# SSD's output product as pairs of blocks in seven products, with h stored and fetched back

## The chip, the cores and the metric

The kernel runs on one core of one Trainium2 chip. The metric is the device time of one execution in microseconds (us), the median of three runs. The profile is that of one execution, taken by the hardware profiler; its times are measured from the start of that execution's span. PE is the matrix engine and PEld its weight load, DVE, ACT and POOL are the vector, scalar and GpSimd engines, and SP is the engine whose queue issues nearly all DMAs here.

## The reference, cut to what matters

One decoder layer over 1024 tokens of width 1024. Two token mixers work on the same normed and modulated input h: a Mamba-2 SSD branch and a differential attention branch. Sigmoid gates merge them, and a gated convolution FFN follows.

```
h = rms_norm(x, pre_norm1_w) * (1.0 + sc1) + sh1
z, xbc, dt_raw, q, k, v, gates = split(h @ w_in)
y_ssd = ssd_branch(z, xbc, dt_raw, ...)         # ends in y * silu(z), group norm, * ssd_norm_w
y_att = diff_attention_branch(q, k, v, ...)     # 16 q and k heads of 64, 8 v heads of 128
gate_ssd, gate_att = split(sigmoid(gates))
merged = gate_ssd * (y_ssd @ w_ssd_o) + gate_att * (y_att @ w_attn_o)
mix = merged @ w_out
```

The product that the change rewrites is y_ssd @ w_ssd_o, 1024 x 1024 by 1024 x 1024. The first 16 of the 64 dimensions of each q and k head are rotated by rope.

## The kernel before, in words

**Numbers in two parts.** Each float32 operand of a large product is a pair: a high part in float32r and a low part, the rest. A product of two pairs is three matmuls (high by high, high by low, low by high). ACT writes the high part, DVE the low one (`split`, lines 93 to 95).

**h.** `hT[k][half]` holds rows 128k to 128k+127 of h transposed, for one half of the tokens (512), high and low side by side: 16 tiles of 512 KB, which stay in SBUF from the first stage to the end of the attention. All large tiles are taken from 43 slots of 4 KB a partition (`Slots`): `get` takes the slot that has been free longest, and a new tile waits until all that was done with the slot's old tile is done.

**Two forms of product.** `block_half` (lines 120 and 121, through `mm3`, lines 113 to 118) multiplies a 128-column block of a weight by h or y for one half of the tokens in 24 matmuls of 512 columns; a block of both halves is 48. The projection of xBC and some others run in `pairs` instead: two blocks of the weight and the halves of the tokens and of the inner dimension form a 2 x 2 product of blocks, done in seven products (Strassen's scheme in Winograd's form) of 12 matmuls each, 84 for two blocks. It needs sums of the weight's quarters (`x_sum`), their high and low parts (`x_split`, issued ahead by `x_ahead`), and seven right sides `HX[...]` from h: b11, b21 and b22 are pieces of h itself, t1 to t4 are differences. `x_mms` issues one product of 12 matmuls; the results are put together in PSUM banks X, Y, Z, by ACT copies and DVE additions.

**The order.** Within a stage the order on PE, DVE, ACT and SP is the order of the code (`tc.manual_schedule`), so each of these engines' instructions, SP's DMAs among them, waits in line. In the attention stage SP is not in that list, and its DMAs are placed by the planner.

**Stages around the change.** From 250 to 344 us z, then to 515 the SSD scan, chunk by chunk in 16 units (`u`), with V's projection (`v_stream`, from line 940) filling PE in between. V's weight comes in two halves of columns of four pieces each; at the switch to the second half `split_v` gives the pieces' high parts, and the low ones come a step later. `sum_dn` runs four steps per unit of W_down's sums in the background, up to unit 11, except for the first two steps of units 7 and 8. `chunk_state` ends a unit: it adds to `prev`, which the next unit's `chunk_out` reads.

Then come the lines that the change rewrites. `seq` is a list of twelve weight blocks: q and k blocks 0 and 1 (the rotated dimensions), then the eight blocks of w_ssd_o. `fetch_seq` loads one, `split_seq` splits it. For each of the four q and k blocks (numbered 0 to 3 in `seq`) PE runs `block_half` for both halves of the tokens; between them, `turn_y` (lines 1179 to 1188) transposes y, which the scan wrote to DRAM (`yd`), 128 columns by 512 tokens at a time through PSUM banks wa, wb, wa, wc in turn, where ACT writes the high part with ssd_norm_w and DVE the low part. y's first half of tokens sits in four tiles `yr`, and the second half is loaded into the same four once the first is transposed. `rope` takes a finished block of q or k: ACT copies it from PSUM, DVE shuffles and multiplies, POOL multiplies, DVE adds, ACT writes the high and DVE the low part, and `store_qk` writes both to DRAM in 16 DMAs on SP.

Then the eight blocks of w_ssd_o (the loop over j): two `block_half` from `yT`, and DVE multiplies the result by the gate (`gth`, loaded from `gsd`), which is stored (`msd`). At j of 3 and 4 `load_qk` fetches the q and k of the first two heads, each in one DMA of 512 KB for q and four of 256 KB for k's high and low part.

The attention starts behind it: `dense_stream` gives PE 24-matmul halves of the other q, k and gate blocks, a step of three matmuls at a time; 14 steps, then the first heads' `scores`, then a fixed mixture of both.

## Time and profile before

| what | value |
|---|---|
| median of 3 runs (lowest to highest) | 1854.49 us (1852.49 to 1855.08) |
| the profiled execution's own time | 1853.7 us |
| its span | 1851.9 us |
| PE busy in the span | 1824.3 us |
| granted TensorE clock | 0.999 |
| DMA, mean over the span | 174 GB/s |

How to read it: rows of a timeline give start and length in us, engine, line, operation, what is written and read, and in brackets how long the engine stood idle before, and what released it. A row of stages gives busy times between two moments. SPq is SP's queue, which issues DMAs; rows of issues give a DMA's size and the time from issue to landing. Matmuls overlap in part, so their distance from start to start is what they cost.

### The profile page before, as it was taken

What the parts mean: (1) busy time and instruction counts of PE and PEld (TensorE: products, weight loads), DVE (VectorE), ACT (ScalarE), POOL (GpSimd) and SP (SyncE); (2) the same over time, 40 slices, a digit from 0 to 9 for tenths busy, and PEclk for the clock granted to TensorE, in tenths of its full rate; (3) what the DMA queues carried; (4) which work ended last, traced back from release to release, by engine and by line L of the source; (5) the groups of instructions that cost most, each with busy time, mean ns of one, the idle gap of its engine ahead of it and who ended that gap; (6) DMA issues with size and microseconds to landing.
All of it is one profiled execution on the core that took longest, in us unless ns stands there. A gap on an engine that the chain in (4) does not pass through costs nothing.

```text
span 1851.9 us, 24405 instructions
## 1 busy us (share of the span) xinstructions
PE 1824.3 (99%) x8974; PEld 1526.9 (82%) x8974; DVE 1292.3 (70%) x1980; ACT 889.3 (48%) x1720; POOL 143.4 (8%) x128
## 2 busy tenths in 40 slices
PE   6999999999999999999999999999999999999998
PEld 4888899987888888888888888888888888888887
DVE  6777867689654257777667464487898888876555
ACT  6644543455532136565556232565545454454542
POOL 0000000255411000000000100000000000000001
PEclk9999999999999999999999999999999999999999
DMA  8365367687646856566734654122333322378754
GB/s 336 130 216 182 102 209 236 222 305 263 239 130 180 253 140 179 155 172 164 194 114 139 236 197 178 51 98 103 102 120 108 103 97 100 108 231 291 247 171 165
DMA packets 130218, 322.57 MB, mean 174 GB/s; under 512 B 14882, under 2 KB 38834, under 8 KB 130099
## 3 DMA queue, kind: packets, MB, share of 16 engines
q1 hardware_dynamic: 129138, 317.86, 52.7%
q0 software_dynamic: 960, 3.15, 0.5%
q8 instruction: 71, 1.16, 0.3%
q14 instruction: 49, 0.39, 0.1%
HBM read 225.79 MB, written 95.17 MB: 173 GB/s over the span
## 4 chain that ended last, share of the span: by engine, by line
PE 86%; DVE 5%; ACT 3%; DMA 3%; issue 1%; SPq 1%; POOL 0%; DVEq 0%; POOLq 0%; ACTq 0%
PE upx L1742 4%; PE upx L1743 4%; PE upx L1741 4%; PE o L1435 3%; PE upy L1742 2%; PE upy L1741 2%; PE upy L1743 2%; PE z L117 2%; PE z L118 2%; PE z L116 2%; PE dx L2105 2%; PE dy L2106 2%; PE dy L2105 2%; PE dy L2104 2%; PE dx L2106 2%; PE at L1422 2%
## 5 line engine op out<-in xcount | busy, mean ns | idle before, releaser
L1741 PE MATMUL upx<-t,wu_t 128*128 128x512 f32 x264 | 103.1, 391 | 0.5 <-DVE cv L2169 0.4
L1742 PE MATMUL upx<-t,wu_t 128*128 128x512 f32 x264 | 102.9, 390 | 0.2 <-DVE t L1859 0.2
L1743 PE MATMUL upx<-t,wu_t 128*128 128x512 f32 x264 | 102.7, 389 | 0.0
L1715 ACT ACTIVATE wu_t<-sab 128x512 fp32r<-128x512 f32 x57 | 34.1, 627 | 128.0 <-DVE sab L1732 128.0
L1423 ACT COPY aT<-at 128x512 f32<-128x512 f32 (+2 forms) x96 | 46.1, 480 | 96.2 <-PE at L1422 96.2
L1435 PEld LDWEIGHTS o<-vt,aT 128*128 128x128 f32 x576 | 75.3, 191 | 9.2 <-ACT aT L1423 4.6
L95 DVE TENSOR_TENSOR g_lo<-gst,g_hi 128x1024 fp32r<-128x1024 f32 (+1 forms) x42 | 47.5, 1135 | 49.1 <-ACT g_hi L94 45.4
L1435 PE MATMUL o<-vt,aT 128*128 128x128 f32 x576 | 80.9, 276 | 0.4 <-ACT aT L1423 0.2
L94 ACT ACTIVATE g_hi<-gst 128x1024 fp32r<-128x1024 f32 (+1 forms) x42 | 41.4, 989 | 63.5 <-DMA gst<-gld_s 35.8
L1396 DVE TENSOR_REDUCE nmx<-sc 128x1 f32<-128x640 f32 (+3 forms) x64 | 65.6, 1024 | 2.2
L1376 PE MATMUL sc<-kst,qst 128*128 128x512 f32 (+2 forms) x192 | 63.8, 341 | 0.0
L1377 PE MATMUL sc<-klo,qst 128*128 128x512 f32 (+2 forms) x192 | 63.3, 346 | 0.0
L1759 DVE SCALAR_TENSOR_TENSOR ug<-cg,vec,ug 128x1023 f32<-128x1023 f32 (+1 forms) x44 | 56.3, 1280 | 6.1 <-ACT ug L1758 5.3
L1741 PEld LDWEIGHTS upx<-t,wu_t 128*128 128x128 f32 x264 | 49.6, 188 | 11.7 <-DVE cv L2169 1.3
L1742 PEld LDWEIGHTS upx<-t,wu_t 128*128 128x128 f32 x264 | 49.6, 188 | 10.6 <-DVE t L1859 0.5
L1743 PEld LDWEIGHTS upx<-t,wu_t 128*128 128x128 f32 x264 | 49.6, 188 | 10.3
L1719 DVE TENSOR_TENSOR wu_t<-sab,wu_t 128x512 fp32r<-128x512 f32 x57 | 39.3, 690 | 26.6 <-ACT wu_t L1715 26.6
L1759 DVE SCALAR_TENSOR_TENSOR uv<-cv,vec,uv 128x1023 f32<-128x1023 f32 (+1 forms) x44 | 56.2, 1277 | 0.9 <-ACT uv L1758 0.9
L1412 DVE RECIPROCAL rsm<-ssum 128x2 f32<-128x2 f32 x64 | 10.6, 165 | 62.5 <-ACT p L1409 35.2
L1414 DVE SCALAR_TENSOR_TENSOR p<-p,coef,p 128x128 f32<-128x128 f32 (+3 forms) x64 | 52.4, 818 | 2.2
L2225 POOL TENSOR_TENSOR rsf<-rsf,nhalf 128x1 f32<-128x1 f32 x8 | 5.2, 656 | 624.8 <-DVE rsf L2224 624.8
L2104 PE MATMUL dx<-wdt_hi,g_hi 128*128 128x512 f32 x132 | 51.3, 389 | 0.0
(537 smaller groups left out, 5919.7 us busy)
## 6 DMA issues: line engine op xcount, KB each, us to landing
adas<-in_w_ada SPq DMA_DIRECT2D x32, 512.0 KB, 5.2
wdr<-in_w_down SPq DMA_DIRECT2D x22, 512.0 KB, 5.8
wtd<-wds SPq DMA_DIRECT2D x22, 512.0 KB, 3.1
wuf<-in_w_up SPq DMA_DIRECT2D x22, 512.0 KB, 3.5
gld_s<-gsum SPq DMA_DIRECT2D x22, 512.0 KB, 2.8
gst<-gld_s SPq DMA_DIRECT2D x20, 512.0 KB, 5.0
wdt_raw<-wtd SPq DMA_DIRECT2D x20, 512.0 KB, 4.9
wuv<-in_w_up SPq DMA_DIRECT2D x19, 512.0 KB, 3.5
```

The lines of the kernel that those rows point to most:

```text
L1376: T.matmul(sc[:, n0:n1], qs_[s][:, tsl], ks_[s][:, n0:n1], start=True, stop=False)
L1377: T.matmul(sc[:, n0:n1], qs_[s][:, tsl], kl[s][:, n0:n1], start=False, stop=True)
L1396: V.reduce_max(nmx[:, bq, s : s + 1], sc[:, :L], axis=AX.X, negate=True)
L1414: V.scalar_tensor_tensor(pr[0][:, :L], pr[1][:, :L], coef[:, bq : bq + 1], pr[0][:, :L], op0=ALU.mult, op1=ALU.add)
L1435: T.matmul(po_of[j, grp][:, qi, :], at[:, k, :], vt[j % 2][:, kt, :], start=(kt == 0), stop=(kt == i))
L1741: T.matmul(out_, wh, xh_, start=(k == 0 and first), stop=False, skip_group_check=not first)
L1742: T.matmul(out_, wh, xl_, start=False, stop=False, skip_group_check=not first)
L1743: T.matmul(out_, wl, xh_, start=False, stop=(k == end), skip_group_check=not first)
L1759: V.scalar_tensor_tensor(u[:, d:], c_[:, : S - d], fw[:, 2 - d : 3 - d], u[:, d:], op0=ALU.mult, op1=ALU.add)
L2104: T.matmul(o, gh[:, kk, tsl], wh, start=(k == 0 and not more), stop=False, skip_group_check=more)
L2105: T.matmul(o, gh[:, kk, tsl], wl, start=False, stop=False, skip_group_check=more)
L2106: T.matmul(o, gl[:, kk, tsl], wh, start=False, stop=(k == KF - 1), skip_group_check=more)
```

## The change

- In xBC's pairs 4 to 6 the twelve tiles of h that have no copy in DRAM are stored to `hd`, one with every other product; the four others have one already.
- At V's second half the low parts come with the next even step instead of the step after the high part. `sum_dn` does nothing in unit 7, and two more steps in units 0 and 1.
- The q and k blocks run in another order of halves (block 3's first half before block 2's second), y's transposes (0 to 7 for the first half of the tokens, 8 to 15 for the second) stand behind them in the order of `turns`, y's second half is loaded into four tiles of its own, and y's pieces b11, b21 (high and low) and the plain pieces y11, y21, y12, y22 take the place of `yT`. From them come t1 to t4 and b22.
- The eight blocks of w_ssd_o become four pairs appended to `pairs`, in seven products each. The gate's multiplication follows the parts of the result as they are ready (`out_so`); its tiles are loaded two at a time.
- Rope of blocks 2 and 3 is cut into steps between the pairs' products, its stores behind the last step.
- h leaves SBUF after the q and k blocks and is loaded back by `h_back` in the last two pairs: three tiles behind product 3 (counted from 0) of the third pair, two behind its product 5, then 4, 4 and 3 behind products 0, 1 and 2 of the last pair. `fetch(0)` and `fetch(1)`, the dense stream's first weights, move from that stream into the last pair, and `load_qk` for the first two heads goes behind product 3 of the last pair.

```diff
+    h_out = [(k, 0) for k in range(KD)] + [(k, 1) for k in range(KH, KD)]
+    hd = {kh: dp.tile([P, S], F32, tag=f"hd{kh[0]}_{kh[1]}", name=f"hd{kh[0]}_{kh[1]}") for kh in h_out}
+    hd |= {(k, 1): h12d[k] for k in range(KH)}
...
+                if 4 <= m < 7 and p % 2 == 0:
+                    k, half = h_out[4 * (m - 4) + p // 2]
+                    SP.dma_start(hd[k, half], hT[k][half].rearrange("p h t -> p (h t)").bitcast(F32))
...
-                    if (vh == 0 and i == 7 and k > 1) or (vh == 1 and i == 0 and k < 2):
-                        if k % 2 == 0:
+                    if k % 2 == 0 and ((vh == 0 and i == 7 and k > 0) or (vh == 1 and i == 0 and k < 4)):
+                        if v_low:
+                            v_low.pop()()
+                            if k == 4 and vh == 0:
+                                v_raw.append(fetch_v(1, 3))
+                        if v_raw:
                             v_low.append(split_v(1, (k // 2 - 1) % 4, v_raw.pop(0)))
...
-        if u not in (7, 8) or n > 1:
+        if u == 7 or (u == 8 and n < 2):
+            return
+        for _ in range(2 if u < 2 and n == 3 else 1):
...
+        if half == 0:
+            n, src = (("b11", y11), ("b21", y21))[c]
+            A.activation(HX[n][kk][:, 0, :], ps, AF.Copy, scale=nw)
+            A.activation(part(src, kk), ps, AF.Copy, scale=nw)
+            lo_of(n, kk, src)
+        elif c == 0:
+            V.scalar_tensor_tensor(part(y12, kk), ps, nw, part(y11, kk), op0=ALU.mult, op1=ALU.subtract)
+        else:
+            A.activation(part(y22, kk), ps, AF.Copy, scale=nw)
...
+    def rope(n, q_):
+        V.stream_shuffle(sw, q_, perm)
+        yield
+        G.tensor_tensor(q_, q_, ropc, op=ALU.mult)
         V.tensor_tensor(sw, sw, rops, op=ALU.mult)
-        V.tensor_tensor(qf, qf, sw, op=ALU.add)
-        split(hi, lo, qf)
-
-    turns = [((0, 1), (2, 3, 4)), ((5, 6, 7), ()), ((0, 1), (2, 3)), ((4, 5), (6, 7))]
+        yield
+        V.tensor_tensor(q_, q_, sw, op=ALU.add)
+        yield
+        A.activation(hi, q_, AF.Copy)
+        yield
+        V.tensor_tensor(lo, q_, hi.bitcast(F32), op=ALU.subtract)
+        yield
+        store_qk(*seq[n], hi, lo)
...
+    def h_back(n):
+        for _ in range(n):
+            half, k = divmod(n_back[0], KD)
+            n_back[0] += 1
+            hT[k][half] = new_hl(f"hb{k}_{half}")
+            SP.dma_start(hT[k][half].rearrange("p h t -> p (h t)").bitcast(F32), hd[k, half])
...
+    turns = {(0, 0): (0, 4, 1), (0, 1): (5, 2, 6), (1, 0): (3, 7, 8, 12), (1, 1): (9, 13, 10), (2, 0): (14, 11, 15)}
...
+        for n, half in ((0, 0), (0, 1), (1, 0), (1, 1), (2, 0), (3, 0), (2, 1), (3, 1)):
+            if half == 0:
+                if n < 2:
+                    fetch_seq(n + 2)
+                ps_of[n] = ps_mm(f"{seq[n][0]}p{seq[n][1]}")
+            block_half(ps_of[n][:, half, :], seq_w[n], hT, half)
+            if (n, half) in ((0, 0), (1, 0), (2, 0)):
+                split_seq(n + 1)
+            if (n, half) == (1, 0):
+                x_load()
+            if half == 0 and n in (1, 2):
+                rope_in(n - 1, qf)
+                old = rope(n - 1, qf)
+                for _ in range(5):
+                    next(old)
+            for i in turns.get((n, half), ()):
+                if i == 8:
+                    SL.put(*yrs[0])
+                    y12, y22 = [[SL.get(f"ys{n_}_{i_}", F32, (P, 2, HALF)) for i_ in range(2)] for n_ in ("12", "22")]
+                turn_y(i % KD, i // KD)
+            if (n, half) == (0, 1):
+                for q in range(4):
+                    SP.dma_start(yrs[1][q], yd[4 + q])
...
+        for m in range(m0, len(pairs)):
+            for p in range(7):
+                if p == 3:
+                    bank["Y"] = ps_wa(f"sy{m}")
+                x_mms(m, p)
...
+                if m > m0 and (m, p) != (m0 + 1, 0):
+                    if next(ropes, True) and m == m0 + 2 and p == 4:
+                        SL.put(hi, lo)
+                if m == len(pairs) - 2:
+                    if p == 3:
+                        SL.put(ropc, rops, qf, qf2, sw)
+                        gthb = [SL.get(f"gthb{i}") for i in range(2)]
+                        for n in range(2):
+                            SP.dma_start(gthb[n], gsd[j + 2 + n])
+                        h_back(3)
+                    elif p == 5:
+                        h_back(2)
+                if last:
+                    if p == 0:
+                        fetch(0)
+                    elif p == 3:
+                        SL.put(*sab)
+                        fetch(1)
+                    SL.put(*HX[order[p][0]])
+                    if p < 3:
+                        h_back((4, 4, 3)[p])
+                    elif p == 3:
+                        qst, kst, klo = [[[SL.get(f"{n}0_{s}", F32R) for s in range(2)]] for n in ("qst", "kst", "klo")]
+                        for i in range(2):
+                            load_qk(i, qst[0][i], kst[0][i], klo[0][i])
...
-        fetch(0)
-        fetch(1)
```

More of the change, by code (lines that the diff above doesn't have):

```diff
@@ L1086, in load_y @@
             SP.dma_start(yr[q], yd[4 * half + q])
-    seq = [("w_q", 0), ("w_k", 0), ("w_q", 1), ("w_k", 1)] + [("w_ssd_o", j) for j in range(8)]
+    seq = [("w_q", 0), ("w_k", 0), ("w_q", 1), ("w_k", 1)]
     seq_w = {}
@@ L1198, in split_seq, with rope_in @@
             split(*seq_w[n], raw)
[L1201 to L1209 removed]
+    def rope_in(n, dst):
+        A.activation(dst, ps_of[n].rearrange("p h t -> p (h t)"), AF.Copy, scale=qscale[seq[n][0]])
@@ new lines, in rope @@
+    def rope(n, q_):
+        V.stream_shuffle(sw, q_, perm)
+        yield
+        G.tensor_tensor(q_, q_, ropc, op=ALU.mult)
+        V.tensor_tensor(sw, sw, rops, op=ALU.mult)
+        yield
[6 more added lines that the diff above has]
+        store_qk(*seq[n], hi, lo)
+    blocks = [(kind, b) for b in (3, 4, 5) for kind in ("w_q", "w_k")] + [("ga", 0)]
@@ new lines, with fetch @@
+    blocks += [(kind, b) for b in (6, 7) for kind in ("w_q", "w_k")] + [("ga", g) for g in range(1, 8)]
+    raws, splits = {}, {}
+    def fetch(n):
+        if n < len(blocks):
+            kind, j = blocks[n]
+            raws[n] = wp.tile([P, KD, P], F32, tag="wraw", name=f"{kind}{j}_raw", bufs=3)
+            SP.dma_start(raws[n].rearrange("p k c -> p (k c)"), a["w_gate"][8 + j] if kind == "ga" else a[kind][j])
+    def h_back(n):
[4 more added lines that the diff above has]
+            SP.dma_start(hT[k][half].rearrange("p h t -> p (h t)").bitcast(F32), hd[k, half])
@@ L1261 @@
+        out_so(1, first, xbank[m]["X"])
+        SP.dma_start(msd[7], cgv[1])
+    SL.put(*gths, *cgv, *evs_x)
+    singles.close()
+    pairs_of_banks = ExitStack()
+    pmm = pairs_of_banks.enter_context(tc.tile_pool(name="pmm3", bufs=1, space=bass.MemoryType.PSUM))
     vt = [SL.get(f"vt{i}", F32, (P, 8, P)) for i in range(2)]
@@ L1275 @@
     sqt = const("sqt", [P, 4])
-    blocks = [(kind, b) for b in (3, 4, 5) for kind in ("w_q", "w_k")] + [("ga", 0)]
-    blocks += [(kind, b) for b in (6, 7) for kind in ("w_q", "w_k")] + [("ga", g) for g in range(1, 8)]
     emitted = {"scores": 0, "values": 0}
-    raws, splits = {}, {}
     finished.clear()
-    def fetch(n):
-        if n < len(blocks):
-            kind, j = blocks[n]
-            raws[n] = wp.tile([P, KD, P], F32, tag="wraw", name=f"{kind}{j}_raw", bufs=3)
-            SP.dma_start(raws[n].rearrange("p k c -> p (k c)"), a["w_gate"][8 + j] if kind == "ga" else a[kind][j])
     def split_later(n):
```

187 lines of the change are left out of this document (128 added, 59 removed).

## The prediction

> **What bounds the kernel now.** I read the page's totals and its chain first, then a table of stages, then the rows of the product itself.
>
> ```profile
> span 1851.9 us, 24405 instructions
> ...
> PE 1824.3 (99%) x8974; PEld 1526.9 (82%) x8974; DVE 1292.3 (70%) x1980; ACT 889.3 (48%) x1720; POOL 143.4 (8%) x128
> ...
> PE 86%; DVE 5%; ACT 3%; DMA 3%; issue 1%; SPq 1%; POOL 0%; DVEq 0%; POOLq 0%; ACTq 0%
> ```
>
> PE is busy for all but 28 us of the span, and 86% of the chain that ended last is PE's: whatever takes matmuls off PE is worth their issue time, and whatever makes PE wait costs the whole wait.
>
> ```profile
> 193.00:212.00 19.00, 19.00 (x86) 15.73 (x85) 16.11 (x20) 10.14 (x16) 0.00 (x0) 1.00 0.37 112
> ...
> 566.00:653.00 87.00, 86.88 (x383) 71.58 (x383) 25.86 (x32) 12.21 (x15) 3.43 (x1) 1.00 0.75 226
> 653.00:664.00 11.00, 11.00 (x53) 9.16 (x52) 2.74 (x5) 0.60 (x1) 0.00 (x0) 1.00 0.12 48
> ```
>
> The columns are the stretch and its length, the busy time of PE, weight load, DVE, ACT and POOL, the clock, the DMA share and GB/s. SSD's output product (566 to 653) keeps PE full, and so does the start of the attention behind it. The first row is one pair of the xBC projection, which already runs in seven products: PE stays full there with DVE busy 16.1 of 19 us, so the pair form itself holds its pace on this chip.
>
> **The product itself.**
>
> ```profile
> L116 PE MATMUL so<-yT,w_ssd_o_hi x128: 387/389/474, 565.5 to 652.4; 128*128 128x512 f32 x128
> ...
> L118 PE MATMUL so<-yT,w_ssd_o_lo x128: 389/389/496, 566.0 to 652.9; 128*128 128x512 f32 x128
> ```
>
> From the first to the last of 128 starts there are 127 steps of three matmuls in 86.9 us, 0.228 us each. Eight blocks of 48 become four pairs of seven products of twelve: 384 matmuls become 336, and 48 x 0.228 = **-10.9 us**. The 64 transposes stay.
>
> **W_v's second half.** Its low parts move one step back, and two steps of W_down's sums leave unit 7.
>
> ```profile
> 436.18 0.50 PE L951 MATMUL v<-wv_lo,hT 128*128 128x512 f32 x1 [0.36 <-DVE wv_lo L938]
> ...
> 438.23 1.13 PE L1032 MATMUL po<-prev,xbcT 128*128 128x512 f32 x2 [1.31 <-DVE prev L1052]
> ```
> ```profile
> 434.90 1.22 DVE L938 TENSOR_TENSOR wv_lo<-wv_raw,wv_hi 128x1024 fp32r<-128x1024 f32 x1 [2.67 <-ACT wv_hi L937]
> 436.04 1.53 DVE L712 TENSOR_TENSOR wds<-wdr 128x512 f32<-128x512 f32 x1
> 437.50 0.68 DVE L1052 TENSOR_TENSOR prev<-pst,prev 128x512 f32<-128x512 f32 x1
> ```
>
> DVE stands still before the last low part, then does the sum, then the state for which PE's next product waits 1.31 us. After the change the state comes before that low part and the sum is gone: **-1.3 us**. Bounds: 0, if the two sums, now in units 0 and 1, cost there what they free here; -1.7 with the 0.36 us too.
>
> **Rope and y's transposes.** Each transpose of y's first half is now emptied by two ACT instructions instead of one, and rope's chain stands ahead of four of them.
>
> ```profile
> 527.28 1.85 ACT L1187 ACTIVATE yT<-ytr,vec 128x512 fp32r<-128x512 f32 x3 [5.09 <-PE ytr L1185]
> 529.01 1.04 ACT L1202 ACTIVATE qf<-w_qp 128x1024 f32<-128x1024 f32 x1
> 536.18 1.06 ACT L94 ACTIVATE thhi<-qf 128x1024 fp32r<-128x1024 f32 x1 [6.13 <-DVE qf L1206]
> ```
> ```profile
> 530.08 1.30 DVE L1203 STREAM_SHUFFLE sw<-qf 128x1024 f32<-128x1024 f32 x1
> ```
> ```profile
> 531.52 3.36 POOL L1204 TENSOR_TENSOR qf<-qf,ropc 128x1024 f32<-128x1024 f32 x1 [12.82 <-issue]
> ```
> ```profile
> 526.64 1.47 PE L1185 MATMUL ytr<-ident,yr 128*128 128x128 f32 x12
> 527.87 0.48 PE L116 MATMUL w_kp<-hT,w_k_hi 128*128 128x512 f32 x1
> ```
>
> Three transposes take PE 1.23 us (526.64 to 527.87), one emptying takes ACT 0.6 (1.85 for three), one half of a block 24 x 0.228 = 5.5. With the first q matmul at 514.8 as now, PE ends block 1's first half at 533.7, four transposes at 535.3, its second half at 540.8. ACT has emptied transposes 5, 2 and 6 by 531.1, splits w_q1 in 1.0 and starts rope at 532.1; by these rows rope's high part starts 7.2 us later (529.01 to 536.18) and frees ACT at 540.3. Only then does ACT empty transpose 3 (done 541.6), then 7 (543.0); DVE empties 8 by 544.4. The three transposes behind block 1's second half want just these three banks: they end at 544.9 instead of 542.0, PE loses **2.9 us**, and block 2 is queued behind them. A second queue runs almost as late, DVE's:
>
> ```profile
> 200.59 0.69 DVE L659 TENSOR_TENSOR xcg<-xz,xevs 128x512 f32<-128x512 f32 x1
> 201.19 0.68 DVE L438 TENSOR_TENSOR xw_b<-xsab,xw_b 128x512 fp32r<-128x512 f32 x1
> ```
>
> A 512-wide DVE step takes 0.60 from start to start. From the end of the second rope, at 555.4 by the same sums, 33 of them stand ahead of the weights of the first pair's fourth product: 555.4 + 19.8 = 575.2, and PE wants them at 576.2. Had PE not lost the 2.9 us, it would lose 2 of them here. Bounds for both together: 2 and 5. In the later pairs DVE has 14 such steps (8.4), the gates' four (2.4) and at most a rope's four double ones (5): 15.8 of 19.1 us, less than the xBC row holds. The gates' loads, issued a pair ahead, wait for nobody. I put these at nothing; without that cover rope's POOL step, 3.4 us, is the price.
>
> **h out and back.** h leaves SBUF to make room for y's pieces. Its 12 stores go into xBC's pairs, where the DMA share is 0.37, and hold SP for no one: nothing; if that cover failed, each would hold a weight by 0.524 MB at the rate below, 1.4 us. The 16 loads back are another matter, and rope 3's 16 stores are put ahead of most of them on SP.
>
> ```profile
> 551.55 0.41 SPq L390 DMA_DIRECT2D khd<-thhi  x1
> 552.02 0.41 SPq L391 DMA_DIRECT2D kld<-thlo  x1
> ```
> ```profile
> khd<-thhi SPq DMA_DIRECT2D x13, 64.0 KB, 2.3
> ```
> ```profile
> 246.00:250.00 4.00, 4.00 (x20) 3.30 (x18) 3.60 (x5) 2.97 (x4) 0.00 (x0) 1.00 0.98 385
> 689.00:695.00 6.00, 6.00 (x36) 5.21 (x36) 4.67 (x11) 4.35 (x16) 1.01 (x1) 1.00 1.04 233
> ```
> ```profile
> 653.09 0.39 PE L1330 MATMUL w_qp<-hT,w_q_hi 128*128 128x512 f32 x1
> ```
> ```profile
> 662.61 0.22 PE L1376 MATMUL sc<-kst,qst 128*128 128x128 f32 x1
> ```
>
> The pairs begin at 568.0 and take 84 x 0.228 = 19.1 each, the last from 625.3 to 644.4. Rope 3's low part stands in the third pair behind its fourth product; DVE gets through it at 619.9. Sixteen stores at 0.46 (551.55 to 552.02) hold SP to 628, and the tiles they read are free for h's fourth and fifth load when they have landed, 2.3 later: 630.3. Behind that wait stand, in this order on SP: two stores of results, a weight, eleven loads of h, a weight, and q and k of the first two heads. Thirteen loads of h, two results and two weights are 17 x 0.524 MB; at 385 GB/s (four tiles of h coming back today, 246 to 250) they take 23.1 us from 631.3, to 654.4. Then two q tiles at that rate, 2.7, and eight loads of k into 64 partitions each, 2.1 MB at 233 GB/s (the row of such loads, 689 to 695), 9.0: all is there at 666.1. The first scores want it 9.5 us after the dense stream starts (653.09 to 662.61), so at 653.9. PE waits **12.2 us** with the whole attention behind it. Bounds: 9, if k's loads run at 385 as well; 16, if rope 3 ends one POOL step later and the list shifts. h itself is in time: its last tile lands at 653, and is wanted at 654.6.
>
> On that rate the Trainium skill differs from the row: "DMA: Bandwidth & Descriptors", section "Where 436 GB/s comes from", has the HBM side bind HBM to SBUF transfers at about 358 GB/s. By it the 17 transfers would take 24.9 us and the wait would be an estimated 14; the measured 385 decides here.
>
> **PE after a long wait.**
>
> ```profile
> 28.44 0.63 PE L242 MATMUL xbc<-hT,wf_lo 128*128 128x512 f32 x1
> 28.87 0.63 PE L243 MATMUL xbc<-hT,wf_hi 128*128 128x512 f32 x1
> ...
> 31.04 0.40 PE L242 MATMUL xbc<-hT,wf_lo 128*128 128x512 f32 x1
> 31.27 0.40 PE L243 MATMUL xbc<-hT,wf_hi 128*128 128x512 f32 x1
> ```
>
> Early in the run, where PE still works between waits, the same matmul stands 0.43 us from the next (28.44 to 28.87), and 0.23 once PE runs through (31.04 to 31.27). If a wait of 12 us brings the first pace back for some 4 us, half of it is lost: **2.0 us**; bounds 0 and 3. The Trainium skill, "TensorE: Matmul & The Clock Gate", section "What's actually happening", says that PE falls to half clock after an idle window of about 3.4 us and needs a busy one as long to come back; by it the price would be an estimated 1.7, and the early rows agree in kind.
>
> **The sum.** -10.9 - 1.3 + 2.9 + 12.2 + 2.0 = **+4.9**. The profiled execution took 1853.7 us (1.8 outside its span), so 1858.6 on its scale; the median of the runs, 1854.49, lies 0.8 above it, which makes **1859.4**. A measurement of this kernel can tell about 0.2%, 3.7 us, from no change: 1850.8 to 1858.2 counts as the same.
>
> **The rivals.** *The heads' loads come in time* (faster). If rope's stores, h and the heads' tiles overlap so that all is in by 654, the last two terms go: 1854.5 - 9.3 = 1845.2. For it: the DMA queue is quiet just behind the product today (share 0.12, 653 to 664), so q and k could have been earlier without harm, and SP may be held less than I count. Against: 23 x 0.524 MB from 630.3 to 653.9 would need 510 GB/s. It decides where the last load of k lands before the dense stream's fifteenth step.
>
> *Half a wait* (no change). If rope 3 ends 3 us sooner than DVE's queue allows by my count and k's loads run at 385, 6 us of wait and 2 of slow pace stay: 1854.5 - 9.3 + 8 = 1853.2.
>
> *The backlog goes on* (slower still). v's tiles, the third weight and the next heads' loads stand behind the same queue; if the values or the next block wait as well, another 8 us: 1867. For it: the DMA share is 0.75 in the product's stage already. Against: those tiles together are less than what the first wait lets through.
>
> **How the numbers follow.** The forecast (a wait of 9 to 16 us with the other bounds, 1854.5 to 1864) has 0.52: 0.33 of it above 1858.2, 0.19 below. In time: 0.28, all of it faster. Half a wait: 0.08, the same. Backlog: 0.12, slower. That makes faster 0.28, same 0.27, slower 0.45. The range of 1844.5 to 1867 leaves out some half of the first rival and of the last, 0.2 in all.
>
> **What would show it.** 336 matmuls at 0.228 in the pairs; a PE wait of 2 to 5 us at y's transposes behind block 1 or in the first pair, none in the other pairs; no PE wait for `prev` near 438; and at the first scores a PE wait of 9 to 16 us, released by DMA into k's low tile, with matmuls 0.43 apart behind it. First scores without a wait make the forecast wrong and the first rival right; a PE wait inside the later pairs makes it wrong in another place.

## The result, and the profile after

| kernel | median (lowest to highest) | ratio to the kernel before, 95% interval |
|---|---|---|
| before | 1854.78 us (1852.49 to 1855.67) | |
| after | 1876.24 us (1873.34 to 1877.8) | 1.0123 (1.011 to 1.0135) |

The change costs 21.5 us where I had forecast 4.9; the time lies 9.2 us above the upper end of my range. The profiled execution of after took 1873.3 us, of before 1853.7. Two experiments below (the earlier ropes with v's tiles last, and rope 2's stores alone) have no profile to compare, since the profiled execution itself was disturbed; only the times of their other executions are used.

The page of after, the same lines as were shown of before, and the row of PE's clock:

```profile
span 1871.5 us, 24483 instructions
...
PE 1823.3 (97%) x8926; PEld 1525.3 (82%) x8926; DVE 1340.7 (72%) x2052; ACT 915.5 (49%) x1776; POOL 141.4 (8%) x128
...
PEclk9999999999999889999999999999999999999999
...
PE 86%; DVE 6%; DMA 4%; ACT 3%; issue 1%; POOL 0%; SPq 0%; DVEq 0%; POOLq 0%; ACTq 0%
```

PE has 48 matmuls fewer and is busy just as long (1824.3 before): what it saved in number it lost in pace (the two 8s in the clock's row), and the span grew by waits. The stages of after, with the same columns as before's:

```profile
515.00:545.00 30.00, 28.20 (x150) 23.39 (x149) 17.48 (x23) 15.51 (x23) 4.08 (x2) 1.00 0.37 103
...
564.00:584.00 20.00, 17.12 (x69) 13.64 (x68) 16.79 (x29) 11.94 (x21) 0.00 (x0) 0.91 0.26 93
584.00:604.00 20.00, 20.00 (x90) 16.57 (x89) 16.84 (x23) 6.71 (x11) 2.40 (x1) 1.00 0.47 170
604.00:624.00 20.00, 16.81 (x69) 13.51 (x68) 17.03 (x21) 6.48 (x11) 2.40 (x1) 0.91 0.57 153
624.00:645.00 21.00, 21.00 (x88) 17.17 (x87) 8.77 (x14) 4.01 (x7) 0.00 (x0) 0.92 0.70 229
645.00:662.00 17.00, 11.01 (x37) 8.55 (x36) 6.99 (x10) 1.74 (x3) 0.00 (x0) 0.80 1.00 383
...
672.00:690.00 18.00, 10.08 (x37) 8.11 (x38) 3.31 (x8) 2.45 (x9) 0.00 (x0) 0.72 0.80 240
```

Only the second pair (584 to 604) runs as before's product did. PE's waits of this stretch, in all, times and the longest:

```profile
PE sc L1549 <- DMA kst<-khd: 7.5, 2, 3.8
PE sy L466 <- ACT yevs L1392: 6.0, 1, 6.0
PE sx L466 <- ACT yevs L1389: 3.2, 1, 3.2
PE sx L466 <- ACT yevs L1373: 2.9, 1, 2.9
PE sc L1550 <- DMA klo<-kld: 2.4, 2, 1.6
PE ytr L1197 <- ACT ys L1202: 1.1, 2, 0.6
PE ytr L1197 <- DVE ys L1205: 0.7, 1, 0.7
```

From the bottom: 1.8 us at y's transposes, 2.9 in the first pair, 3.2 in the third, 6.0 in the last, and 9.9 at the first scores. PE's timeline shows what a wait brings with it, and where PE goes on for good:

```profile
572.50 0.69 PE L466 MATMUL sx<-yt,xw_t 128*128 128x512 f32 x1 [2.88 <-ACT yevs L1373]
572.99 0.63 PE L467 MATMUL sx<-yt,xw_t 128*128 128x512 f32 x1
573.41 0.63 PE L468 MATMUL sx<-yt,xw_t 128*128 128x512 f32 x1
...
660.35 0.39 PE L1503 MATMUL w_qp<-hb,w_q_hi 128*128 128x512 f32 x1
...
681.11 0.45 PE L1550 MATMUL sc<-klo,qst 128*128 128x128 f32 x1 [0.83 <-DMA klo<-kld]
681.35 0.73 PE L1503 MATMUL w_qp<-hb,w_q_hi 128*128 128x512 f32 x1
```

Against before, the product starts 1.5 us earlier (564.0, 565.5 before), the dense stream 7.3 later (660.35, 653.09 before), and PE goes on behind the first scores 18.4 later (681.35; 663.00 before). Behind that, nine more matmuls stand 0.43 apart, which is 1.9 us. The two make 20.3; the spans differ by 19.6, so the rest of the kernel takes the same time. SP's timeline shows what the loads did (start, length, what is written and read):

```profile
609.57 0.33 SPq L1411 DMA_DIRECT2D msd<-scg  x1
609.94 0.42 SPq L391 DMA_DIRECT2D qd<-thhi  x1
...
622.56 1.87 SPq L1254 DMA_DIRECT2D hb<-hd  x3
624.69 0.32 SPq L394 DMA_DIRECT2D khd<-thhi  x1
625.95 0.32 SPq L395 DMA_DIRECT2D kld<-thlo  x1
...
637.72 0.42 SPq L395 DMA_DIRECT2D kld<-thlo  x1
641.98 0.34 SPq L1528 DMA_DIRECT2D vt<-vd  x1
642.49 0.81 SPq L1254 DMA_DIRECT2D hb<-hd  x2
643.34 0.43 SPq L1411 DMA_DIRECT2D msd<-scg  x1
```

Rope 3's sixteen stores take from 624.7 to 638.1, and then SP stands until 642 in front of one load of v (`vt`, L1528). It belongs to the attention, whose SP instructions the planner places, and it put this one ahead of h's fourth tile. SP's waits name what it waits for, and what slowed the stores:

```profile
SPq L1528 <- PE sy L468: 3.8, 1, 3.8
...
SPq L395 <- DMA hb<-hd: 1.9, 2, 1.0
...
SPq L394 <- DMA hb<-hd: 1.4, 1, 1.4
...
SPq L395 <- DMA gthb<-gsd: 1.0, 1, 1.0
```

The load of v waits for a matmul of the last pair's fourth product (by the kernel's order of slots, the one that it gets holds a piece of y until then). The first eight stores wait for the landing of the gates' and h's loads issued before them. The last reading concerns DVE:

```profile
622.24 1.22 DVE L1234 TENSOR_TENSOR thlo<-qf,thhi 128x1024 fp32r<-128x1024 f32 x1
...
650.58 0.69 DVE L1380 TENSOR_TENSOR scg<-sz,yevs 128x512 f32<-128x512 f32 x1 [13.22 <-DMA msd<-scg]
```

In the last pair DVE cannot write `cg` until the third pair's store has read it; that store stands behind the load of v, so DVE stood 13.2 us and PE 6.0.

### The profile page after: what moved, and what is told of

It reads as the page before. It is cut to its first block, busy times and chain, and to the rows that moved or that the text cites. A ratio compares the mean times of both kernels' runs of the same rounds, so it can differ in the third digit from the quotient of the medians.

```text
span 1871.5 us, 24483 instructions
## 1 busy us (share of the span) xinstructions
PE 1823.3 (97%) x8926; PEld 1525.3 (82%) x8926; DVE 1340.7 (72%) x2052; ACT 915.5 (49%) x1776; POOL 141.4 (8%) x128
## 4 chain that ended last, share of the span: by engine, by line
PE 86%; DVE 6%; DMA 4%; ACT 3%; issue 1%; POOL 0%; SPq 0%; DVEq 0%; POOLq 0%; ACTq 0%
PE upx L1915 4%; PE upx L1914 4%; PE upx L1916 4%; PE o L1608 3%; PE dx L2278 2%; PE dx L2279 2%; PE dx L2277 2%; PE upy L1916 2%; PE upy L1914 2%; PE upy L1915 2%; PE z L117 2%; PE z L118 2%; PE z L116 2%; PE dy L2278 2%; PE dy L2279 2%; PE dy L2277 2%
## 5 line engine op out<-in xcount | busy, mean ns | idle before, releaser
L1916 PE MATMUL upx<-t,wu_t 128*128 128x512 f32 x264 | 102.7, 389 | 0.0
L1916 PEld LDWEIGHTS upx<-t,wu_t 128*128 128x128 f32 x264 | 49.6, 188 | 10.3
L1503 PE MATMUL gap<-hb,ga_hi 128*128 128x512 f32 x128 | 56.5, 441 | 0.0
L2398 POOL TENSOR_TENSOR rsf<-rsf,nhalf 128x1 f32<-128x1 f32 x8 | 5.2, 655 | 623.5 <-DVE rsf L2397 623.5
```

Of the source, the lines that this page charges most:

```text
L1503: T.matmul(ps, w[0][:, k, :], xh_, start=(k == 0), stop=False)
L1916: T.matmul(out_, wl, xh_, start=False, stop=(k == end), skip_group_check=not first)
```

## The experiments

The product starts between 564.0 and 567.8 in the profiles of the changed kernels, so I compare distances from its first matmul: to the dense stream's start (D), and to the matmul with which PE goes on behind the first scores (G). That mark has a fault. In 1, 6, 7, 14 and 16 the three short waits at y's transposes (0.5 to 0.7 us each, as in after) brought seven or eight matmuls some 0.43 apart, and the product starts 1.6 us later; in 1, 6 and 7 the first pair's wait is then 1.3 to 1.4 us instead of 2.9. D and G look up to 1.6 us too short there. Q is free of this: it runs from the first matmul of the q and k blocks (510.87 in after) to the same end as G. All three come from PE's timelines. Times are medians; the kernel before took 1852.9 to 1853.4 beside them.

| kernel | time | ratio, 95% interval | D | G | Q |
|---|---|---|---|---|---|
| before | | | 87.6 | 97.5 | 148.2 |
| after | 1876.2 | 1.0123 (1.011 to 1.0135) | 96.3 | 117.3 | 170.5 |
| 1 second tile for cg | 1876.9 | 1.0125 (1.011 to 1.014) | 92.0 | 116.2 | 171.0 |
| 2 b22 later | 1874.8 | 1.012 (1.0103 to 1.0137) | 93.1 | 115.0 | 168.2 |
| 3 rope's multiplication on DVE | 1875.8 | 1.0121 (1.0107 to 1.0134) | 95.6 | 117.3 | 170.5 |
| 4 rope 2's stores earlier | 1873.5 | 1.0109 (1.0093 to 1.0124) | | | |
| 5 30 dense steps first | 1877.9 | 1.0131 (1.0116 to 1.0146) | 96.9 | | |
| 6 ropes earlier | 1883.7 | 1.016 (1.0145 to 1.0175) | 101.0 | 125.1 | 180.0 |
| 7 first heads' v by hand | 1878.0 | 1.0133 (1.0119 to 1.0147) | 94.1 | 117.5 | 172.3 |
| 8 6 and 7 | 1881.2 | 1.0156 (1.0141 to 1.0172) | 102.7 | 123.4 | 176.6 |
| 9 v's tiles last | 1873.8 | 1.0109 (1.0094 to 1.0124) | 92.6 | 116.0 | 169.2 |
| 10 6 and 9 | 1872.2 | 1.01 (1.0083 to 1.0116) | | | |
| 11 6, 7, 2, h earlier | 1869.0 | 1.0083 (1.007 to 1.0097) | 87.5 | 111.5 | 164.7 |
| 12 6, 9, 2, h earlier, halves of q and k | 1863.8 | 1.0056 (1.0039 to 1.0072) | 87.3 | 105.1 | 158.3 |
| 13 12 and 24 dense steps first | 1877.9 | 1.0131 (1.0115 to 1.0146) | 87.7 | | |
| 14 12, 1, 3 | 1862.7 | 1.0051 (1.0037 to 1.0064) | 81.7 | 102.3 | 157.1 |
| 15 1, 2, 9, halves, both ropes' stores earlier | 1865.4 | 1.0065 (1.0051 to 1.0078) | 84.5 | 105.9 | 159.1 |
| 16 15 and 3 | 1863.9 | 1.0056 (1.0042 to 1.0069) | 81.9 | 103.0 | 157.7 |
| 17 before, V and sums alone | 1850.2 | 0.9985 (0.9976 to 0.9994) | | | |
| 18 before, h's stores alone | 1852.9 | 0.9999 (0.999 to 1.0008) | | | |

**Waits in the pairs, one at a time (1 to 4).** The theories: each wait costs by itself (B), or the loads set the end and a wait matters only as far as it moves them (A).

```diff
# 1
                             SL.put(*gths)
                             gths = gthb
+                            cg_old = cg
+                            cg = SL.get("scg2")
+                            cgv = [cg, cv]
```

> The last pair gets a tile of its own for the first half of its result (cg), so that DVE need not wait until the third pair's store has read the old one; nothing else changes. In the profile of the changed kernel that wait costs PE 6.0 us and slow matmuls behind it. Theory A, the loads of h, q and k set the end: the wait goes, the dense stream starts some 8 us earlier (at 652), but the last k tile still lands at about 681, so PE waits that much longer for h or at the first scores, and the time stays within 2 us of the changed kernel (1873 to 1877). Theory B, each wait costs by itself: 8 us less, 1865 to 1868.

Measured: no change in time. The dense stream starts 4.3 us earlier by D, of which 1.6 is the mark's fault (`cv`, stored in the same way, holds DVE and so PE for 4.9 us next), and by Q PE goes on no earlier, 171.0 for 170.5: the wait at the first scores grows instead, to 10.3 and 2.6. The 6 us at `cg` lay beside the wait for the loads. A holds.

```diff
# 2
                     x_ahead(m, 3)
-                    if m == m0:
-                        for k in range(KH):
-                            hi_of("b22", k, y22)
-                            lo_of("b22", k, y22)
-                        SL.put(*y22)
                 elif p == 1:
...
                     if m == m0:
+                        for k in range(KH):
+                            hi_of("b22", k, y22)
+                            lo_of("b22", k, y22)
+                        SL.put(*y22)
                         cg, cv = cgv = [SL.get(f"sc{n}") for n in "gv"]
```

> In the first pair the parts of b22 (four ACT and four DVE steps) stand behind product 1's evacuation and weights instead of ahead of them, so ACT copies bank X before them. Theory: the first pair's wait of 2.9 us with 1.9 us of slow matmuls is ACT's order alone and goes; everything behind it, rope 3's stores and the loads included, moves up with it: 4 to 5 us less, 1869 to 1872. Rival, DVE's queue is as late: the wait moves to the weights of the fourth or fifth product, or the end stays where the loads put it: within 1.5 us of the changed kernel.

Measured: the first pair's wait is gone, G is 2.3 us better, the time 1.4 (the intervals overlap). ACT's order was the cause of that wait, but half of the gain went into the next ones: the third pair's wait grew from 3.2 to 4.4 and one of 1.5 came in the second.

```diff
# 3
-        G.tensor_tensor(q_, q_, ropc, op=ALU.mult)
+        (G if n < 2 else V).tensor_tensor(q_, q_, ropc, op=ALU.mult)
```

> The changed kernel with one edit: the multiplication of ropes 2 and 3 that POOL does (2.4 us, beside which a DVE step of 0.68 took 2.73) is done by DVE (1.2 us). Theory: DVE's queue in the third pair was late by that stretch, so ACT copied bank X late and PE waited 3.2 us with 3 us of slow matmuls behind it; that wait lies ahead of the last pair's fourth product, so it is in series with the loads, and goes in full: 3 to 6 us less than the changed kernel, 1870 to 1873. Rival, DVE is full in the pairs with or without POOL: within 1.5 us of it, 1875 to 1878.

Measured: 3.0 us of wait in the third pair (3.2 before the edit), the same time. POOL was not what held it. ACT's timeline of this kernel names another holder:

```profile
620.06 1.06 ACT L1232 ACTIVATE thhi<-qf 128x1024 fp32r<-128x1024 f32 x1 [2.91 <-DMA qd<-thhi]
621.02 0.57 ACT L1389 COPY yevs<-sx 128x512 f32<-128x512 f32 x1
```

Rope 3's high part is written into the tile from which rope 2's stores still read, and the copy of bank X, for which PE waits, is next in ACT's line.

```diff
# 4
         V.tensor_tensor(lo, q_, hi.bitcast(F32), op=ALU.subtract)
+        if n == 2:
+            store_qk(*seq[n], hi, lo)
         yield
-        store_qk(*seq[n], hi, lo)
+        if not (n == 2):
+            store_qk(*seq[n], hi, lo)
```

> The changed kernel with one edit: rope 2's 16 stores stand one product earlier on SP, right behind its low part and ahead of the second pair's store of cg, which waits for DVE. In the changed kernel they go out from 609.9 to 617.8, and ACT, which must write rope 3's high part into the same tile, starts it at 619.5, with the copy of bank X behind it. New theory after DVE's version of the multiplication changed nothing: it is these stores that hold ACT, not DVE. The stores are then out by 614 and landed by 617, the third pair's wait of 3.2 us falls below 1 us and its 3 us of slow matmuls go; since this lies ahead of the last pair's fourth product, SP's load of v and all of h behind it move up too: 4 to 6 us less than the changed kernel, 1870 to 1872. Rival, DVE's addition at 618.9 is as late as the stores: within 1.5 us of it.

Measured: 2.8 us less than after, and the intervals overlap; without a profile the wait itself can't be read. See 15 and 16 for the same step in other company.

**More dense work first (5, 13).** `NFIRST` goes from 20 to 36, and from 20 to 30.

> 30 instead of 14 steps of the dense stream stand ahead of the first scores (NFIRST 36 for 20; the same steps are missing later, spread over the 64 heads' items). Theory A, the loads set the end only through the first scores: the waits there (10 us, and 2 us of slow matmuls) go, 1862 to 1865. Rival: the attention needs these steps as filling later, and the gain is given back, 1870 or more.

> As the run with halves of columns, and 24 instead of 14 steps of the dense stream ahead of the first scores, 6.8 us of matmuls. If the loads of q and k are what PE waits for, the wait shrinks by 6.8 us or to nothing: 1855 to 1858. If the wait only moves (to the next weight, as with 30 steps in the changed kernel): 1862 or more.

Measured: no gain in 5 (1877.9), and 13 is 14 us worse than 12. The steps that come first want their own weights, which stand in the same queue. ACT's timeline of 13:

```profile
665.67 1.15 ACT L1478 ACTIVATE w_k_hi<-w_k_raw 128x512 fp32r<-128x512 f32 x2 [15.21 <-DMA w_k_raw<-in_w_k]
...
681.12 1.15 ACT L1478 ACTIVATE w_q_hi<-w_q_raw 128x512 fp32r<-128x512 f32 x2 [13.33 <-DMA w_q_raw<-in_w_q]
```

ACT stands for the second and for the third weight, with the scores' own ACT steps behind it. In 13 PE waits 3.3 us at a dense step, 4.7 at its first step behind the scores and 4.1 for the next heads' k instead: the rival that the wait only moves was right, though not all of the 14 us was traced. In 5 the time is the rival's, but what the profile shows is not its lost filling: PE waits 6.9 us at a dense step, behind ACT and the third weight.

**The order on SP (6 to 10).** In these texts theories A and C have the order of SP's list hold the loads up, and B has the rate of the DMAs alone set the end.

```diff
# 6
-                if m > m0 and (m, p) != (m0 + 1, 0):
-                    if next(ropes, True) and m == m0 + 2 and p == 4:
+                if (m, p) >= (m0, 5):
+                    if next(ropes, True) and m == m0 + 2 and p == 1:
```

> All steps of ropes 2 and 3 stand three products earlier (from product 5 of the first pair instead of product 1 of the second), so rope 3's 16 stores stand ahead of the gates' and h's loads on SP and the two tiles they read come free some 10 us earlier. Theory A, the loads set the end and rope 3's stores hold them up: the stores are issued in 7 to 8 us instead of 13, the gap in the loads from 636 to 645 closes, the third pair's store goes out in time too, so the wait for cg goes as well: 12 to 18 us less, 1858 to 1864. Theory B, the DMA rate itself is the limit (h, q and k at about 400 GB/s from the third pair on): at most 4 us less.

> In the changed kernel SP's list holds one load of v (the first heads' values, 64 KB) ahead of h's fourth tile; the planner put it there from the attention stage. It waits for PE's third product of the last pair, and h's loads and the third pair's store stand behind it. Here the eight loads of v stand last in the hand-ordered stage; nothing else changes. Theory C, this load holds SP's queue: h's fourth tile goes out as soon as rope 3's stores have landed, at about 640 instead of 642.5, and all later loads with it: 2 to 3 us less than the changed kernel, 1873 to 1874. Theory B, the DMA rate alone sets the end: nothing changes.

> Ropes 2 and 3 three products earlier, as in the run before that was slower for it, and the loads of v last in the hand-ordered stage. In that run SP stood from 631 to 643.8 in front of the one load of v, and every load of h behind it. Theory C (that load was what made the earlier rope useless): the loads of h go out from about 631, the store of cg by 638, the wait for cg is gone and the waits at the first scores are under 4 us: 1856 to 1863. Theory B, the rate of the DMAs sets the end whatever SP's order: 1873 or more.

Measured: 6 is 7.5 us slower than after, and 7 and 8 (with the first heads' eight loads of v at the end of the ordered list) bring nothing. All three miss what theory A or C put, and the reason is in SP's list: with the first heads' loads out of the way the planner put the first load of the next heads' v (L1530) into the same place. So 7 and 8 did not do what their texts say. SP's wait in 8, and the stages behind it:

```profile
SPq L1530 <- PE sy L468: 13.3, 1, 13.3
```
```profile
632.00:636.00 4.00, 4.00 (x19) 3.32 (x18) 4.00 (x6) 1.01 (x2) 0.00 (x0) 1.00 0.00 0
636.00:640.00 4.00, 4.00 (x20) 3.30 (x19) 0.86 (x2) 1.15 (x2) 0.00 (x0) 1.00 0.00 0
640.00:644.00 4.00, 4.00 (x19) 3.33 (x18) 0.00 (x0) 1.12 (x2) 0.00 (x0) 1.00 0.01 2
644.00:648.00 4.00, 2.23 (x10) 1.50 (x8) 0.00 (x0) 0.00 (x0) 0.00 (x0) 1.00 0.94 333
```

For 13.3 us SP waits with all loads of h behind it, and from 632 to 644 the DMAs move nothing (the last column, GB/s). The loads that follow take what they take. From v's load to PE's going on it is 39.4 us in after (641.98 to 681.35), 39.5 in 1 (643.68 to 683.23), 39.2 in 2 (640.44 to 679.66), 39.8 in 3 and 40.8 in 7: different waits, nearly one distance. In 6 and 8 five more tiles stand behind it, and it is 48.6 and 45.3.

Then only the slots were changed: v's two tiles are taken last of the attention's tiles.

```diff
# 9
-    vt = [SL.get(f"vt{i}", F32, (P, 8, P)) for i in range(2)]
...
     gev = SL.get("gev", F32, (P, 2, HALF))
+    vt = [SL.get(f"vt{i}", F32, (P, 8, P)) for i in range(2)]
```

> The changed kernel with one edit: the two tiles of v are taken last among the attention's tiles, so they lie in other slots, and no load of v stands ahead of h's in SP's list any more (moving the first heads' loads did not do that: the next heads' load took the place). Theory C, the list's order: h's loads go out when rope 3's stores have landed, some 2 us earlier than now, and PE goes on behind the first scores that much earlier: 1.5 to 2.5 us less than the changed kernel. Theory B, the rate alone: no change.

> Ropes 2 and 3 three products earlier, and v's tiles taken last. Theory C: SP no longer stands 13 us in front of a load of v with the DMAs at rest; h's loads and the gates' start at about 632, the third pair's store goes out by 640 and the wait for cg shrinks below 3 us; PE goes on behind the first scores 45 us (five tiles more than in the changed kernel) after the first of these loads, at about 677 instead of 688 to 692: 10 to 13 us less than with the earlier ropes alone, 1868 to 1873. Theory B, nothing but the rate: as before, 1880 or more.

Measured: 9 gains 1.4 us in G and 2.5 in time, as theory C said, though the intervals overlap; in its SP timeline no load of v stands ahead of h's any more. 10 settles the price: the same edit takes 11.5 us off kernel 6, with intervals far apart. The earlier ropes, 7.5 us of loss by themselves, are 1.6 us faster than 9 with it, and these intervals overlap: that they gain anything is not shown.

**What is left is the rate (11, 12).** 11 has 6, 7 and 2, and takes the first three tiles of h behind rope 3's stores, two products earlier; 12 has 9 for 7, and loads q and k of the first two heads in two halves of columns.

```diff
# 11
+                        SL.put(ropc, rops, qf, qf2, sw, hi, lo)
+                        h_back(3)
# 12
-                        for i in range(2):
-                            load_qk(i, qst[0][i], kst[0][i], klo[0][i])
+                        for c in (slice(0, HALF), slice(HALF, S)):
+                            for i in range(2):
+                                load_qk(i, qst[0][i], kst[0][i], klo[0][i], c)
```

> As the run with the earlier ropes and v last, and also b22's parts behind product 1's evacuation, and the first three loads of h two products earlier (behind rope 3's stores in the third pair). Theory A with C, the loads set the end and the order on SP sets the loads: no wait over 2 us in the pairs, at most 3 us at the first scores: 1845 to 1854, level with the kernel before or faster. If PE still waits 6 us or more at h's tiles or the scores, the DMA rate is the limit: 1858 or more.

> Ropes earlier, b22 later, h's first loads two products earlier, v's tiles last, and q and k of the first two heads loaded in two halves of columns: the first scores need only the first half, so 1.6 MB of loads move behind them. In the run with the same order without the halves PE waited 12.8 us at the first scores while the DMAs ran at 220 to 300 GB/s. Theory B for what is left (rate): 1.6 MB at 250 GB/s, 5 to 7 us less than that run's 1869: 1862 to 1864. Rival: the wait at the first scores counts for the whole tile, or a load of half rows takes as long as one of whole rows: 1868 to 1870.

Measured: 11 has no load of v in the way and is 7.2 us faster than after, but PE still waits 12.8 us at the first scores, so its first expectation fell and its second (the rate) holds. 12 takes another 5.2 us off, and PE's wait at the first scores falls to 6.6 us. The wait goes with the bytes that stand ahead of the scores.

**All together (14 to 16).**

> The run with halves of columns (1863.8), with ropes' multiplication on DVE and a second tile for the last pair's first half. If POOL's step makes the waits in the second pair (3.0, 2.0 and 1.8 us there) and the store of cg the 2.2 us in the last, both go: 1855 to 1860. If the loads' rate sets the end, the wait at the first scores grows by what the last pair gains, and only the second pair's part is kept at best: 1859 to 1864.

> The pieces that the runs so far favour, with ropes where the change has them: both ropes' stores right behind their low parts (rope 3's so ahead of the gates' and h's loads), b22 later, v's tiles last, a second tile for cg, q and k of the first heads in halves of columns. If the waits in the pairs are the stores', the pairs lose under 3 us, and the loads run at full rate from about 625: 1853 to 1859. If the loads' rate still holds the first scores by 6 us or more: 1859 to 1863.

> The run with all the pieces (1865.4), with ropes' multiplication on DVE as well: one edit. There the stores are out of ACT's way and rope 3's high part starts 0.1 us behind DVE's addition, and PE still waits 3.3 us in the third pair. Theory: DVE's queue was the second holder, nearly level with the stores, which is why neither edit alone did anything; now POOL's stretch (2.0 us) goes and DVE's own step (1.2 us) comes, the wait falls to 2 us or less, and rope 3's stores and all loads behind them move up: 2 to 4 us less, 1861 to 1864. Rival, DVE stays full: no change, 1865.

Measured: 1862.7, 1865.4 and 1863.9. 14's stages behind its third pair:

```profile
632.00:640.00 8.00, 8.00 (x37) 6.60 (x36) 3.46 (x6) 2.86 (x5) 0.00 (x0) 1.00 0.94 350
640.00:648.00 8.00, 8.00 (x37) 6.64 (x36) 3.75 (x5) 1.74 (x3) 0.00 (x0) 1.00 1.03 414
648.00:656.00 8.00, 8.00 (x37) 6.64 (x36) 1.36 (x3) 0.00 (x0) 0.00 (x0) 1.00 1.03 410
656.00:664.00 8.00, 2.37 (x8) 0.99 (x7) 0.23 (x1) 0.89 (x2) 0.00 (x0) 0.82 0.97 292
```

The dense stream of 14 starts 14.6 us earlier than after's by D (13.0 with the mark's fault taken off), PE is full from 632 to 656, and it still waits 8.4 us at the first scores and 2.6 for v's tile behind them, with the DMAs at 350 to 414 GB/s until q's and k's loads, during which they move 292. Q stays 8.9 us behind before's 148.2, and the time 9.3. Where the ropes stand as in the change, the third pair's wait outlived every edit (with the earlier ropes such a wait stands in the second pair, 1.8 us in 14): in 15 the stores are out of the way and ACT starts rope 3's high part when DVE's addition ends,

```profile
619.73 1.06 ACT L1232 ACTIVATE thhi<-qf 128x1024 fp32r<-128x1024 f32 x1 [1.43 <-issue]
```
```profile
618.42 1.22 DVE L1230 TENSOR_TENSOR qf<-qf,sw 128x1024 f32<-128x1024 f32 x1
```

with 3.3 us of wait for PE, and in 16, with POOL out of it as well, it is 2.8. So rope 2's stores and DVE's line seem to hold ACT almost equally long, and PE, which comes earlier by then, wants what either edit frees. That ACT's copy ahead of rope's high part would end it was not tried.

**Parts of the change on the kernel before (17, 18).** The edits are the change's own lines for `split_v` and `sum_dn`, and the stores to `hd`.

> The kernel before with only V's second half and W_down's sums as in the change. By the traces PE gains 2.5 us in the stretch from 400 to 450: 1.3 to 2.5 us less than the kernel before. Rival: the two sums that moved to units 0 and 1, or a wait behind them, give it back: no change.

> The kernel before with the twelve stores of h in xBC's pairs, as in the change, and nothing else. Step of the prediction: they cost nothing, since the DMAs are idle two thirds of that stage: within 1 us of the kernel before. Rival: each holds a weight's load behind it on SP by 1.4 us: up to 17 us more.

Measured: V's second half with the sums moved gives 2.65 us (ratio 0.9985, 0.9976 to 0.9994), and is faster than both kernels; it is the version to keep. Its row of the stretch, where before had PE busy 47.31:

```profile
400.00:450.00 50.00, 49.94 (x279) 40.26 (x278) 44.94 (x60) 29.74 (x77) 30.37 (x21) 1.00 0.82 289
```

The twelve stores of h cost nothing (0.9999, 0.999 to 1.0008).

## Why the prediction was wrong, step by step

**The product itself, -10.9:** right. Where nothing holds it, a pair takes 19.0 us (587.9 to 606.9, the second).

**W_v, -1.3 (bounds 0 and -1.7):** the direction was right, the size was not: -2.65. The waits of before in that stretch have a third row, for a tile on the same DVE line, that I had not read:

```profile
PE pst L1050 <- DVE tt L1033: 1.0, 2, 0.7
```

It went with the 1.31 and the 0.36 of my two rows, 2.7 in all.

**The turns and the first pair, +2.9 (2 to 5):** the place and the waits were right, 1.8 us at the transposes and 2.9 in the first pair, 4.7 in all. I had taken them for alternatives, and in after both came; they trade in part, since in 1, 6 and 7, where the product starts 1.6 us later, the second is 1.3 to 1.4. In after 1.7 us of slow matmuls behind the second were not in the term. ACT's order, four high parts of b22 ahead of one copy, was the mechanism (2), not the fourth product's weights.

**Pairs 2 to 4 at nothing:** wrong. I compared DVE's busy time with a pair's length (15.8 of 19.1 us) and found room. What decides is the order in line and who may overwrite what: rope 3's high part stands ahead of ACT's copy of bank X and waits for DVE and for rope 2's stores (3.2 us, and 3.0 of slow matmuls; that this is near the 3.4 of POOL's step, my price without the cover, is luck, since 3 takes that step off POOL and the wait stays), and `cg` has one tile, whose store stands on SP behind everything else (6.0, and 2.9 of slow matmuls).

**h's stores at nothing:** right (18).

**The wait at the first scores, +12.2 (9 to 16):** the mechanism was right, but that its size nearly was (9.9) is luck: the same loads landed 15.0 us later than I put them, at 681.1 instead of 666.1, and PE was late by about as much, so the wait hides its own error. This is the step that failed: *DVE gets through rope 3's low part at 619.9, sixteen stores hold SP to 628, and the tiles are free at 630.3*. Measured: 623.5, 638.1 and 642.5. Of these 12.2 us, 3.6 are rope 3 (7.6 us later behind the product's start, with the stalls of the first and third pair ahead of it, less the 4.0 by which the product started before my 568.0), 6.5 the stores, which took 14.6 us instead of 8.1 because each of the first eight waits for a load of half a megabyte ahead of it (in 15, where they stand ahead of the gates' and h's loads, all but the first are some 0.46 apart), and 2.1 the load of v, which I did not know to be there. The transfer from there I had put at 35.8 us; it took 38.6.

**So the sum.** 15.0 us of later landing is what my forecast lacks: 1858.6 on the profile's scale, and 1873.3 measured, 14.7 more. The waits inside the pairs are no sum of their own. Those ahead of the last pair's fourth product moved the loads and counted through them (2.3 us in 2, by G and by Q); that at `cg` lay beside the loads' time and counted nothing (1).

**Slow matmuls, +2.0:** 1.9 behind the first scores, as put, and 7.6 more in the pairs, of which the same is true.

**The rivals.** That the loads come in time was wrong at every rate measured. Half a wait failed on its condition: rope 3 ended 3.6 us later than my count, not 3 sooner. The backlog that I priced at 8 us was nearest in time (1867), but not by its mechanism: in after no wait behind the first scores grew. In 12 and 14, where PE comes there earlier, one for v's tile appears (2.0 and 2.6 us).

On the rate, "DMA: Bandwidth & Descriptors", section "Where 436 GB/s comes from", of the Trainium skill has the HBM side bind such loads at about 358 GB/s; 410 and 414 GB/s over eight microseconds each (14) do not agree with it, and the measurement decides.

## What to carry to other kernels

A tile sent out and fetched back is paid where it comes back: add up the bytes that must land between the first free slot and the first use, and put the loads on the queue's own list, with every instruction that stands ahead of them and what it waits for. A load that a planner has placed can stand in front of a list that you ordered by hand; read the list as compiled, since a wait there costs nothing to its own tile and everything to those behind it. When two waits end at the same load, mending the first shows nothing: measure from a common mark to the point where the engine goes on for good, as with Q here, and not by the sum of the waits. The mark must lie ahead of every wait that can differ, or it moves with them, as D's and G's did.

## What the runs showed of the hardware

- **The slow pace behind a wait keeps a clock of its own.** After 2.88 and 3.19 us of waiting in after, eight and fourteen matmuls followed 0.42 to 0.59 apart. In 15, after 3.28 us, the first came at the full pace and only then eight slow ones:

```profile
621.31 0.50 PE L466 MATMUL sx<-yt,xw_t 128*128 128x512 f32 x1 [3.28 <-ACT yevs L1394]
...
622.58 0.40 PE L468 MATMUL sx<-yt,xw_t 128*128 128x512 f32 x1
622.80 0.60 PE L466 MATMUL sx<-yt,xw_t 128*128 128x512 f32 x1
623.20 0.63 PE L467 MATMUL sx<-yt,xw_t 128*128 128x512 f32 x1
```

  In 12 a wait of 3.05 us brought none; one of 2.02 brought eight in 6, none in 12, and in 8 slow ones only 1.6 us after PE had gone on (608.93, 610.56). The Trainium skill, "TensorE: Matmul & The Clock Gate", section "What's actually happening", has a free-running window of about 3.4 us decide. The late start and the scatter agree with that; an idle time as long as the window was not needed here.
- **Stores of 64 KB behind loads of 512 KB go at the loads' pace:** the first eight of rope 3's in after are 1.3 to 1.7 us apart (624.69 to 634.13), the others 0.46, as where no load is ahead.
- **Loads of q and k keep the DMAs full at a lower rate:** 292 GB/s in 14 (656 to 664) with the DMAs' share at 0.97, and 242 in after (668 to 674) with it at 1.04, against 410 and 414 in 14 for the stretch ahead of them, mostly h's. k's loads go into 64 partitions each and q's, like h's, into 128; that this is the reason was not tested apart.
